# Rotary embedding on one core: the first batch loaded in eight transfers of 16 partitions, and one row of eight moved from TensorE to VectorE

## The chip, the cores and the metric

The kernel runs on one core of a Trainium2 chip. The metric is the device time of one execution in microseconds (us), as the median of several executions. A run is slow when it lies over 1.5% above the fastest of the same kernel.

## The reference, cut to what matters

```python
batch, seq, dim = (16, 512, 1024)            # num_heads = 16, so head_dim 64
x = x.reshape(batch, seq, num_heads, head_dim)
x1, x2 = x[..., :32], x[..., 32:]
rotated = concatenate([x1 * cos - x2 * sin, x1 * sin + x2 * cos], axis=-1)   # fp32
```

The cosine and sine tables are [512, 32]. Input and output are 33.5 MB each, so 67 MB have to move between HBM (the chip's main memory) and SBUF (the core's working memory, 128 partitions), and there is little arithmetic on each byte.

## The kernel before

One batch is one tile: partition p holds the four positions 4p to 4p+3, which is 4096 numbers, 16 KB in one piece of memory. A ring holds ten batches (40 rows of 1024 numbers per partition; "row of work", or unit `u`, below). SyncE issues the loads, ScalarE's queue issues the stores.

```python
PE2 = [u % 2 == 1 for u in range(NU)]        # rows whose two products TensorE adds
V2 = [u % 8 == 3 for u in range(NU)]         # rows whose sine product VectorE makes
# ... (cut)
xv = x.rearrange("b (p r) d -> b p (r d)", r=R)       # R = 4

def on_sync(sp):
    for c in range(NC):
        if c * R >= RING:
            sp.wait_ge(sem_out[c - RING // R], 16)
        sp.dma_start(tile(c), xv[c]).then_inc(sem_in[c], 16)
        if c == 0:
            # the cosine and sine tables, one transfer each (cut)

def on_scalar(ae):
    # tables (cut)
    for u in range(NU):
        c, r, k = where(u)
        if PE2[u]:
            ae.wait_ge(sem_e, n_pe[u])
            ae.activation(xs[:, k, :], t1_ps[:, u % NT1, :], COPY).then_inc(sem_a, 1)
        if r == R - 1:
            wait_added(ae, u)
            ae.dma_start(ov[c], tile(c)).then_inc(sem_out[c], 16)
    for c in range(NC):
        ae.wait_ge(sem_out[c], 16)
```

VectorE multiplies each row of work by the cosine into PSUM (the memory that matmuls add into). GpSimd (VectorE for one row in eight) multiplies the row with its halves swapped by the signed sine into SBUF. The two products are added either by TensorE, as an identity matmul onto the product in PSUM with a copy back by ScalarE, or by VectorE ("comb").

## Time and profile before

| | before |
|---|---|
| median | 162.7 us (162.4 to 163.02, 4 runs) |
| span in the profile | 161.2 us |
| first 16 KB row starts to move | 1.80 us |
| 4096 rows of 611 ns over 16 DMA engines | 156.4 us |
| first load: first row starts, last row ends | 1.80 us, 8.24 us |
| first load, mean of its 128 rows | 717 ns |

A "row" in this table, and in all that follows about transfers, is one 16 KB piece of one partition, the unit in which the DMA engines work here; its times come from the trace's records of single DMA pieces, which do not name the engine. They stand on the clock of the profile. 611 ns a row is 26.8 GB/s for one engine, 429 GB/s for sixteen.

The first two parts of the page of the kernel before. The strings of digits are the busy tenths in 40 slices of 4.03 us; the last line is what the DMA engines moved in each slice:

```profile
span 161.2 us, 678 instructions
PE 83.3 (52%) x134; PEld 27.6 (17%) x134; DVE 122.0 (76%) x108; ACT 34.5 (21%) x35; POOL 130.4 (81%) x62
DVE  0079296998999999969998997976969588796000
POOL 1059999999999999999999993998939989399000
DMA  5999999999999999999999999999999999999995
GB/s 159 404 450 427 427 439 386 398 447 419 431 451 411 439 451 396 451 431 413 447 415 439 443 415 439 447 402 443 423 431 447 411 439 443 413 443 431 419 439 236
```

The engines of the DMA are busy from the second slice to the last but one, while VectorE and GpSimd have holes. So the time is set by the transfers: what counts is when the first row starts, how long each row takes, and whether the engines ever run dry.

The stretches of the first 20 us of the same kernel. The columns are the stretch, its length, the busy time and count of instructions of TensorE's matmuls, TensorE's weight loads, VectorE, ScalarE and GpSimd, the granted clock of TensorE, the DMA share, and GB/s. A row counts whole in the stretch in which it starts, which is why a share can be over 1:

```profile
0.00:5.00 5.00, 2.74 (x6) 0.74 (x6) 0.27 (x1) 1.28 (x1) 0.70 (x6) 1.00 0.66 213
5.00:10.00 5.00, 0.00 (x0) 0.00 (x0) 1.02 (x4) 0.51 (x2) 0.29 (x1) 1.00 1.01 416
10.00:15.00 5.00, 0.49 (x1) 0.50 (x2) 5.00 (x5) 0.00 (x0) 5.00 (x3) 1.00 1.02 436
15.00:20.00 5.00, 5.00 (x7) 1.85 (x6) 2.13 (x3) 1.02 (x1) 5.00 (x3) 1.00 1.01 433
```

The timeline of the start (start, duration, engine, line, operation). The SPq lines are issues of transfers; the first vector copy waits for the cosine table, whose 512-byte pieces start only as the last rows of the first load end (first piece at 7.24 us, last row's end at 8.24 us):

```profile
0.80 0.37 SPq L123 DMA_DIRECT2D x_sb<-in_x_dram  x1
1.22 0.43 SPq L126 DMA_DIRECT2D stage<-in_cos_dram  x1
1.70 0.42 SPq L126 DMA_DIRECT2D stage<-in_sin_dram  x1
8.95 0.29 DVE L202 COPY tab_ps<-stage 128x128 f32<-128x128 f32 x1 [7.75 <-DMA stage<-in_cos_dram]
```

And the end of it, the last copy and the issue of the last store:

```profile
152.35 1.02 ACT L139 ACTIVATE x_sb<-t_ps 128x1024 f32<-128x1024 f32 x1 [5.01 <-PE t_ps L164]
153.41 0.34 ACTq L142 DMA_DIRECT2D out_dram<-x_sb  x1
```

The first row of that store moves at 154.59 us, 1.18 us after the issue began and with no gap behind the store before it: taken in order, its sixteen first rows start within 4 ns of the ends of that store's sixteen last rows. At the start of the kernel the first row moved 1.00 us after its issue began (0.80 to 1.80 us), so the tail has hardly any slack: an estimate from these two is 0.2 us.

### The profile page before, as it was taken

Reading aid. Unit: us, or ns where it says so; the run is one execution under the profiler, and the core shown is the slowest. Engines: PE = TensorE matmul, PEld = TensorE weight load, DVE = VectorE, ACT = ScalarE, POOL = GpSimd, SP = SyncE. Lnnn points to the kernel's source line nnn. Section 1 sums busy time; section 2 is a strip of 40 time slices with the busy share of each in tenths; the row PEclk is TensorE's granted clock in tenths of the full one; section 3 lists DMA queues with packets and bytes.
Section 4 is the critical chain, followed back from the end, with each engine's and each line's share of the span. In section 5 each row is a group of like instructions: output and inputs, shape, how many; then the busy total and the mean of one; then the engine's idle time right before and its main releaser. Section 6 shows DMA issues by size and latency. Waiting matters only on the chain.

```text
span 161.2 us, 678 instructions
## 1 busy us (share of the span) xinstructions
PE 83.3 (52%) x134; PEld 27.6 (17%) x134; DVE 122.0 (76%) x108; ACT 34.5 (21%) x35; POOL 130.4 (81%) x62
## 2 busy tenths in 40 slices
PE   6004949239463665692639444284490784643700
PEld 1002313113121221121212111021120121210100
DVE  0079296998999999969998997976969588796000
ACT  3010222222222222222222222204031203122200
POOL 1059999999999999999999993998939989399000
PEclk9999987995999999579995999959779559789585
DMA  5999999999999999999999999999999999999995
GB/s 159 404 450 427 427 439 386 398 447 419 431 451 411 439 451 396 451 431 413 447 415 439 443 415 439 447 402 443 423 431 447 411 439 443 413 443 431 419 439 236
DMA packets 4900, 67.28 MB, mean 417 GB/s; under 512 B 544, under 2 KB 800, under 8 KB 800
## 3 DMA queue, kind: packets, MB, share of 16 engines
q1 hardware_dynamic: 2592, 33.69, 49.8%
q10 hardware_dynamic: 2304, 33.56, 48.6%
q8 instruction: 1, 0.02, 0.0%
q14 instruction: 3, 0.02, 0.0%
HBM read 33.69 MB, written 33.55 MB: 417 GB/s over the span
## 4 chain that ended last, share of the span: by engine, by line
POOL 27%; DVE 20%; issue 18%; PE 17%; ACT 5%; DMA 5%; another core or an unknown queue 2%; SPq 0%; DVEq 0%; POOLq 0%
POOL t_sb L193 27%; PE t_ps L164 17%; DVE x_sb L235 9%; DVE t_ps L224 8%; DMA stage<-in_sin_dram 5%; ACT x_sb L139 4%; DVE t_sb L215 3%; SPq L126 0%; SPq L123 0%; ACT s_sb L133 0%; ACT s_sb L134 0%; POOLq L115 0%; DVEq L221 0%; DVEq L234 0%
## 5 line engine op out<-in xcount | busy, mean ns | idle before, releaser
L193 POOL TENSOR_TENSOR t_sb<-x_sb,s_sb 128x1024 f32<-128x1024 f32 x56 | 129.7, 2350 | 17.7 <-DMA x_sb<-in_x_dram 9.4
L164 PE MATMUL t_ps<-t_sb,ident 128*128 128x512 f32 x128 | 80.5, 768 | 67.8 <-DVE t_ps L224 46.3
L224 DVE TENSOR_TENSOR t_ps<-x_sb,tab_ps 128x1024 f32<-128x1024 f32 x64 | 76.6, 1226 | 17.1 <-DMA x_sb<-in_x_dram 8.6
L139 ACT ACTIVATE x_sb<-t_ps 128x1024 f32<-128x1024 f32 x32 | 32.7, 1023 | 111.0 <-PE t_ps L164 111.0
L164 PEld LDWEIGHTS t_ps<-t_sb,ident 128*128 128x128 f32 x128 | 26.9, 231 | 120.8 <-DVE t_ps L224 75.9
L235 DVE TENSOR_TENSOR x_sb<-t_ps,t_sb 128x1024 f32<-128x1024 f32 x32 | 39.0, 1218 | 0.0
L215 DVE TENSOR_TENSOR t_sb<-x_sb,tab_ps 128x1024 f32<-128x1024 f32 x8 | 9.7, 1211 | 0.0
L202 DVE COPY tab_ps<-stage 128x128 f32<-128x128 f32 x1 | 0.3, 295 | 7.8 <-DMA stage<-in_cos_dram 7.8
L150 PE MATMUL t_ps<-zero 128*128 128x512 bf16 x6 | 2.7, 630 | 1.3 <-DVE zero L198 1.3
L133 ACT ACTIVATE s_sb<-stage 128x128 f32<-128x128 f32 x1 | 0.3, 309 | 7.0 <-DMA stage<-in_sin_dram 7.0
L133 ACT ACT_TABLE_LOAD x1 | 1.3, 1283 | 0.8 <-PEq L268 0.8
L150 PEld LDWEIGHTS t_ps<-zero 128*128 128x128 bf16 x6 | 0.7, 138 | 2.3 <-DVE zero L198 1.2
L198 DVE MEMSET zero<- 128x256 uint32 x1 | 0.3, 272 | 0.9 <-PEq L268 0.9
L175 POOL MEMSET ident<- 128x128 f32 x1 | 0.2, 204 | 0.3 <-POOLq L268 0.3
L177 POOL TENSOR_SCALAR_AFFINE_SELECT ident<-ident 128x128 f32<-128x128 f32 x1 | 0.3, 292 | 0.1
L268 POOL MEMSET const-float32-0.0<- 128x1 f32 x1 | 0.1, 98 | 0.3 <-issue 0.3
L134 ACT ACTIVATE s_sb<-stage 128x128 f32<-128x128 f32 x1 | 0.3, 293 | 0.0
L204 DVE TENSOR_SCALAR tab_ps<-stage 128x128 f32<-128x128 f32 x1 | 0.3, 284 | 0.0
L205 DVE COPY tab_ps<-stage 128x128 f32<-128x128 f32 x1 | 0.3, 284 | 0.0
L268 POOL MEMSET const-bfloat16-1.0<- 128x1 bf16 x1 | 0.1, 101 | 0.0
L268 POOL MEMSET const-uint8-127<- 128x1 uint8 x1 | 0.1, 101 | 0.0
L268 POOL MEMSET const-float32-1.0<- 128x1 f32 x1 | 0.1, 98 | 0.0
## 6 DMA issues: line engine op xcount, KB each, us to landing
x_sb<-in_x_dram SPq DMA_DIRECT2D x16, 2048.0 KB, 53.6
out_dram<-x_sb ACTq DMA_DIRECT2D x16, 2048.0 KB, 22.1
stage<-in_cos_dram SPq DMA_DIRECT2D x1, 64.0 KB, 7.7
stage<-in_sin_dram SPq DMA_DIRECT2D x1, 64.0 KB, 7.4
```

The costliest lines, as they stand in the source:

```text
L133: ae.activation(s_sb[:, :, 0, :], sv, COPY, scale=-1.0)
L134: ae.activation(s_sb[:, :, 1, :], sv, COPY).then_inc(sem_s, 1)
L139: ae.activation(xs[:, k, :], t1_ps[:, u % NT1, :], COPY).then_inc(sem_a, 1)
L150: pe.matmul(t1_ps[:, k, b * BANK:(b + 1) * BANK], zero[:, 0:P], zero[:], start=True, stop=True).then_inc(sem_w, 1)
L164: ins = pe.matmul(t1_ps[:, u % NT1, b * BANK:(b + 1) * BANK], ident[:], t2[:, b * BANK:(b + 1) * BANK], start=False, stop=True, skip_group ...
L177: pl.affine_select(out=ident[:], in_=ident[:], compare_op=mybir.AluOpType.is_equal, fill=0.0, base=0, pattern=[[-1, P]], channel_multiplier=1,
L193: pl.tensor_tensor(t2_sb[:, u % NT2, :, :, :], swapped(k), sin_of(s_sb, r), mult).then_inc(sem_p, 1)
L198: ve.memset(zero[:], 0.0).then_inc(sem_z, 1)
L215: ve.tensor_tensor(t2_sb[:, u % NT2, :, :, :], swapped(k), sin_of(s_ps, r), mult).then_inc(sem_d, 1)
L224: ve.tensor_tensor(t1_ps[:, u % NT1, :].rearrange("p (h d) -> p h d", d=HALF), x_sb[:, k, :, :, :].rearrange("p h t d -> p (h t) d"), c_ps ...
L235: ve.tensor_tensor(xs[:, k, :], t1_ps[:, u % NT1, :], t2_sb[:, u % NT2, :, :, :].rearrange("p h t d -> p (h t d)"), add,).then_inc(sem_v, 1)
L268: nc = _bacc.Bacc("TRN2", target_bir_lowering=False, num_devices=1)
```

## The change

The intent: in the first load of before, the first rows take 731 to 1944 ns instead of 611. The author's guess was that this comes from engines that start 64 KB or more apart in memory. Cut into eight transfers of 16 partitions, each engine is taken to get one row of each transfer, so that the engines begin 16 KB apart. Rows added by TensorE fall from four of eight to three, so that the last row of every second batch, the last batch among them, no longer passes through TensorE and ScalarE. The sixteen final waits become one, for the ten stores that nothing else waits for.

```diff
-    PE2 = [u % 2 == 1 for u in range(NU)]
+    PE2 = [u % 8 in (1, 3, 6) for u in range(NU)]
...
+    FIRST = 8
...
-                sp.dma_start(tile(c), xv[c]).then_inc(sem_in[c], 16)
-                if c == 0:
+                if c > 0:
+                    sp.dma_start(tile(c), xv[c]).then_inc(sem_in[c], 16)
+                else:
+                    for j in range(FIRST):
+                        ps = slice(j * P // FIRST, (j + 1) * P // FIRST)
+                        sp.dma_start(tile(c)[ps], xv[c, ps]).then_inc(sem_in[c], 16)
...
-                    ae.dma_start(ov[c], tile(c)).then_inc(sem_out[c], 16)
-            for c in range(NC):
-                ae.wait_ge(sem_out[c], 16)
+                    ae.dma_start(ov[c], tile(c)).then_inc(sem_out[c] if c < len(sem_out) else sem_rest, 16)
+            ae.wait_ge(sem_rest, 16 * (NC - len(sem_out)))
...
-                pl.wait_ge(sem_in[c], 16)            # and the same on VectorE
+                pl.wait_ge(sem_in[c], 16 if c else 16 * FIRST)
```

More of the change, by code (lines that the diff above doesn't have):

```diff
@@ L70, in bass_split_heads_rope_kernel @@
         sem_in = [stack.enter_context(nc.semaphore(f"in{c}")) for c in range(NC)]
-        sem_out = [stack.enter_context(nc.semaphore(f"out{c}")) for c in range(NC)]
+        sem_out = [stack.enter_context(nc.semaphore(f"out{c}")) for c in range(NC - RING // R)]
+        sem_rest = stack.enter_context(nc.semaphore("rest"))
         sem_cos = stack.enter_context(nc.semaphore("cos"))
@@ L211, in mul @@
                 if r == 0:
-                    ve.wait_ge(sem_in[c], 16)
+                    ve.wait_ge(sem_in[c], 16 if c else 16 * FIRST)
                 if V2[u]:
```

## The prediction

> **What bounds it now.** The transfers. The page's slice row shows the 16 DMA engines at 9 tenths or more from the second slice to the one before last, at 417 GB/s mean; by stretch, the DMA share is 1.00 to 1.01 from 10 to 154 us. VectorE (122.0 us busy) and GpSimd (130.4 us) have slack overall; the chain of waits names them, but that chain is not the limit while the queues hold work. In the trace's packet records nearly every 16 KB row takes 611 ns; 4096 rows x 611 ns / 16 engines = 156.4 us. The first row starts at 2.2 us, so the floor is near 158.7 us of a 161.2 us span. The other 2.5 us are: (a) the first load, whose 128 rows take 717 ns on average, the very first rows 731 to 1944 ns, which is 0.85 us per engine, about 1.0 on the engine that ended last; (b) the rows read at 24 to 28 us, as the first store begins, about 0.5 us; (c) the rest: table rows, semaphore writes, one engine ending about 1 us after the mean.
>
> **What the change touches.**
> 1. First load in eight: seven more issues at about 0.43 us each (the table issues took 0.42 to 0.43 us on SyncE's queue). One issue feeds each engine a 611 ns row, so issue stays ahead. Aim: remove (a). At most 0.85 to 1.0 us; I expect 0.6 if it works. Added: 7 semaphore writes per engine, 9 ns each, about 0.06 us.
> 2. Rows added by TensorE, from four of eight to three: ScalarE copies fall from 32 to 24, VectorE adds rise from 32 to 40, +8 x 1.22 = +9.8 us, to about 132 us. Per batch VectorE needs about 8.5 us, GpSimd 8.2 us, against 9.7 us of transfer. Still hidden. At the end the last store was issued at 153.41 us, its first row moved about 1.6 us later, just as the engines ran free: hardly 0.2 us of slack. The last row now goes through a VectorE add (1.22 us) instead of a matmul group and copy (3.4 + 1.0 us), so I expect that issue 2 to 3 us earlier, which keeps the tail filled if the start gains.
> 3. One final wait: only the last store's wait counted. About 0.
>
> **The risk.** [...] No run of before shows a 16-partition transfer. I give this a quarter: the rest of the change (freeing the tail) makes sense only if the start gets shorter.
>
> **Prediction.** [...] I say 162.4 us, 8 in 10 within 161.0 to 169.5. Faster by over 2%: 0.02; within 2%: 0.72; slower: 0.26.
>
> **What would show it.** Right: the first load's rows average under 660 ns; table landings near 8 us; DMA share 9 tenths throughout; last store issue near 150.5 us; VectorE near 132 us. Wrong: first-load rows of 1 to 2.4 us for several rounds, a low GB/s in slices 2 to 4, and everything after shifted by the same amount; or VectorE falling behind after 100 us, a hole in the transfers after the last load.

The forecast came to 162.4 us, the upper end of 161.8 to 162.4 us, its range for a first load that isn't slowed.

## The result, and the profile after

The changed kernel takes 174.5 us (174.21 to 174.73, 4 runs) against 162.7 us: a ratio of 1.0724, with a 95% interval from 1.0692 to 1.0756. It is slower by 11.8 us. A ratio in this text is the mean time of one kernel's fast runs over that of the other's of the same rounds, so it isn't quite the ratio of the medians.

The first two parts of the page of the changed kernel, 4.31 us a slice:

```profile
span 172.5 us, 614 instructions
PE 84.1 (49%) x102; PEld 26.0 (15%) x102; DVE 131.4 (76%) x116; ACT 26.4 (15%) x27; POOL 130.3 (76%) x62
DVE  0000195799999997999789997999899969996900
POOL 1000099999999999999999999499884989399100
DMA  8999899999999999999999999999999999999996
GB/s 122 122 122 122 205 429 426 426 429 426 426 426 437 433 429 448 427 426 429 429 427 422 426 441 429 433 445 429 433 429 426 426 426 433 433 429 437 437 429 270
```

Read the last two lines together. The DMA engines count as busy from the start, but in the first four slices they move 122 GB/s instead of about 430. A busy DMA engine isn't a fast one: its row simply takes longer (2092 ns on average in the first load, 717 ns before). Everything after the fifth slice runs at the rate of before.

Its stretches:

```profile
0.00:5.00 5.00, 2.74 (x6) 0.74 (x6) 0.27 (x1) 1.28 (x1) 0.70 (x6) 1.00 0.80 115
5.00:10.00 5.00, 0.00 (x0) 0.00 (x0) 0.00 (x0) 0.00 (x0) 0.00 (x0) 1.00 1.06 125
10.00:15.00 5.00, 0.00 (x0) 0.00 (x0) 0.00 (x0) 0.00 (x0) 0.00 (x0) 1.00 1.09 128
15.00:20.00 5.00, 0.00 (x0) 0.00 (x0) 0.00 (x0) 0.00 (x0) 0.00 (x0) 1.00 0.89 111
```

Its timeline at the start. The eight issues take 3.62 us in all, so issue isn't what holds the first load up; the tables, whose first piece starts at 18.09 us, as the load's last rows end (18.09 to 19.19 us), come 11.9 us later than before (the first copy at 20.83 against 8.95 us):

```profile
0.80 3.62 SPq L131 DMA_DIRECT2D x_sb<-in_x_dram  x8
4.46 0.42 SPq L133 DMA_DIRECT2D stage<-in_cos_dram  x1
4.92 0.43 SPq L133 DMA_DIRECT2D stage<-in_sin_dram  x1
20.83 0.29 DVE L208 COPY tab_ps<-stage 128x128 f32<-128x128 f32 x1 [19.63 <-DMA stage<-in_cos_dram]
```

And its end:

```profile
163.26 1.02 ACT L146 ACTIVATE x_sb<-t_ps 128x1024 f32<-128x1024 f32 x1 [5.05 <-PE t_ps L170]
164.32 0.34 ACTq L149 DMA_DIRECT2D out_dram<-x_sb  x1
```

The trace's records of single rows give the sum. The excess over 611 ns, added up and divided by 16 engines, is the engine time lost:

| engine time lost (us per engine) | before | after |
|---|---|---|
| first load | 0.85 | 11.85 |
| second load | 0.00 | 0.39 |
| fifth load (beside the start of the first store) | 0.53 | 0.01 |
| all rows of the kernel | 1.55 | 12.42 |

The difference of the last line is 10.9 us, of the 11.3 us by which the span grew. From the end of the first load to the end of the span both kernels take nearly the same: 161.22 - 8.24 = 153.0 us before, 172.48 - 19.19 = 153.3 us after. The loss is in the first load. The end of a row's record is not yet its landing: the last semaphore increment of the first load came 0.45 us after it before (8.69 us), and 1.43 us after it in the changed kernel (20.62 us).

### The profile page after: what moved, and what is told of

It is laid out like the page before. It is cut to its first block, busy times and chain, and to the rows that moved or that the text cites. A ratio compares the mean times of both kernels' runs of the same rounds, so it can differ in the third digit from the quotient of the medians.

```text
span 172.5 us, 614 instructions
## 1 busy us (share of the span) xinstructions
PE 84.1 (49%) x102; PEld 26.0 (15%) x102; DVE 131.4 (76%) x116; ACT 26.4 (15%) x27; POOL 130.3 (76%) x62
## 4 chain that ended last, share of the span: by engine, by line
DVE 38%; PE 21%; issue 15%; DMA 9%; ACT 6%; POOL 3%; SPq 2%; DVEq 0%
PE t_ps L170 21%; DVE x_sb L241 18%; DVE t_ps L230 15%; DMA stage<-in_sin_dram 9%; ACT x_sb L146 6%; DVE t_sb L221 4%; POOL t_sb L199 3%; SPq L131 2%; SPq L133 0%; ACT s_sb L140 0%; ACT s_sb L141 0%; DVEq L229 0%; DVEq L240 0%; DVEq L227 0%
## 5 line engine op out<-in xcount | busy, mean ns | idle before, releaser
L230 DVE TENSOR_TENSOR t_ps<-x_sb,tab_ps 128x1024 f32<-128x1024 f32 x64 | 77.0, 1226 | 12.1 <-ACT x_sb L146 10.4
L241 DVE TENSOR_TENSOR x_sb<-t_ps,t_sb 128x1024 f32<-128x1024 f32 x40 | 48.6, 1218 | 0.0
L170 PEld LDWEIGHTS t_ps<-t_sb,ident 128*128 128x128 f32 x96 | 25.3, 289 | 133.4 <-DVE t_ps L230 87.6
L146 ACT ACTIVATE x_sb<-t_ps 128x1024 f32<-128x1024 f32 x24 | 24.6, 1024 | 118.2 <-PE t_ps L170 118.2
L140 ACT ACT_TABLE_LOAD x1 | 1.3, 1283 | 0.8 <-PEq L274 0.8
```

The source lines that it names most:

```text
L140: ae.activation(s_sb[:, :, 0, :], sv, COPY, scale=-1.0)
L170: ins = pe.matmul(t1_ps[:, u % NT1, b * BANK:(b + 1) * BANK], ident[:], t2[:, b * BANK:(b + 1) * BANK], start=False, stop=True, skip_group ...
L230: ve.tensor_tensor(t1_ps[:, u % NT1, :].rearrange("p (h d) -> p h d", d=HALF), x_sb[:, k, :, :, :].rearrange("p h t d -> p (h t) d"), c_ps ...
L241: ve.tensor_tensor(xs[:, k, :], t1_ps[:, u % NT1, :], t2_sb[:, u % NT2, :, :, :].rearrange("p h t d -> p (h t d)"), add,).then_inc(sem_v, 1)
```

## The experiments

Four theories stood at first. **A**: the set of partitions to which a load writes at one time sets how long its rows take, whether these are neighbours or not (the prediction's risk). **B**: engines that read memory 16 KB apart get in each other's way in HBM. **C**: eight small transfers cost more than one, in issues and semaphore writes. **D**: the limit is per block of neighbouring partitions.

This table is the core of the evidence, from the row records: the mean row of the first load in ns, by rounds of 16 rows in order of their start.

| kernel | how the first load is cut | round 1 | round 2 | round 4 | round 8 |
|---|---|---|---|---|---|
| before | whole | 1307 | 705 | 621 | 613 |
| after | 8 x 16 neighbouring partitions | 1378 | 2159 | 2199 | 2201 |
| e3_rows_apart | the same, memory 128 KB apart | 1209 | 2013 | 2052 | 2052 |
| e4_stride4 | 8 x every fourth partition, memory as in after | 1014 | 1068 | 1183 | 1190 |
| e6_four32 | 4 x 32 neighbouring partitions | 992 | 1213 | 1283 | 1281 |
| e7_two64 | 2 x 64 neighbouring partitions | 830 | 1212 | 1273 | 1275 |

### e1_whole: undo the cut, keep the rest

```diff
-    FIRST = 8
+    FIRST = 1
```

> The changed kernel with its first load put back into one transfer of 128 partitions; the row split (three of eight) and the single final wait stay. Every theory that blames the way the first load is cut expects the time of before, 162.7 us within 0.5, first-load rows near 717 ns. If the row split or the single wait cost something of their own, this run stays above 163.5 us. If the freed tail is worth anything, it is up to 0.5 us under before.

Measured: 162.39 us (5 runs) against 162.59 us, ratio 0.9984 (0.9972 to 0.9997). The cut alone makes the loss. The row split and the single wait together are worth 0.16%, and the run doesn't tell which of the two gives it. It is the fastest version of all, but by so little that it counts as the same. Its GB/s line and its last issue:

```profile
GB/s 143 404 453 424 436 436 367 432 441 408 453 420 432 445 412 438 428 428 449 402 449 432 420 449 412 441 432 416 453 424 428 441 408 453 424 428 449 404 449 281
152.38 0.34 ACTq L149 DMA_DIRECT2D out_dram<-x_sb  x1
```

The start is that of before. The last store is issued at 152.38 us, 1.0 us earlier than before, not the 2 to 3 us of the prediction. The last row of the batch no longer waits for TensorE, but the row before it still does: its matmuls (3.68 us, from 147.61 us) and the copy after them, which ends at 152.35 us, now come last.

### e2_only_eight: the cut alone, on the kernel before

```diff
-                sp.dma_start(tile(c), xv[c]).then_inc(sem_in[c], 16)
+                    for j in range(8): ...     # as in the change; waits for 16 * 8 on batch 0
```

> The kernel before with only the first load cut into eight transfers of 16 partitions. If the cut alone makes the loss: 174.5 us within 0.7, first-load rows near 2100 ns. If the loss needs the fuller VectorE too, clearly less, 165 to 172 us.

Measured: 174.32 us (4 runs), ratio 1.072 (1.0701 to 1.0739), rows of the first load 2101 ns on average. The loss is there without the row split.

### e3_rows_apart: the same partitions, other memory addresses

```diff
-                        sp.dma_start(tile(c)[ps], xv[c, ps]).then_inc(sem_in[c], 16)
+                        sp.dma_start(tile(c)[ps], xv[c, j::FIRST]).then_inc(sem_in[c], 16)
```

> The changed kernel, eight transfers to the same blocks of 16 partitions, but each fetches every eighth row of memory, so the engines read 128 KB apart instead of 16 KB (batch 0 comes out wrong on purpose). Theory A[...]: nothing changes, rows near 2200 ns, 174.5 us. Theory B, engines that read 16 KB apart collide in HBM: rows fall to 620 to 750 ns, about 163 us. Theory C, cost of many small transfers: 174.5 us.

Measured: 173.15 us once, rows at 2052 ns (batch 0 wrong). Theory B falls: with 128 KB between the engines' addresses the rows are 7% shorter, not 70%. In this one trace addresses have a small part in it; the partitions hold the large one. Its GB/s line starts as slowly as that of the changed kernel:

```profile
GB/s 122 126 122 120 297 429 429 425 432 436 436 432 432 432 429 432 432 427 429 429 427 429 429 432 429 432 432 429 432 432 432 440 429 432 432 432 429 432 432 264
```

### e4_stride4: the same memory addresses, other partitions

```diff
-                        sp.dma_start(tile(c)[ps], xv[c, ps]).then_inc(sem_in[c], 16)
+                        p0 = 64 * (j // 4) + j % 4
+                        sp.dma_start(tile(c)[p0:p0 + 61:4], xv[c, ps]).then_inc(sem_in[c], 16)
```

> The changed kernel, eight transfers that read the same memory as in the changed kernel (16 rows in a row each) but write to every fourth partition of one half: partitions 0,4,..,60 and so on (batch 0 wrong on purpose). Theory A: [...] half the time per row: about 1100 ns, first load near 9 us, total about 166 us. Theory B and theory C: 2200 ns and 174.5 us as before this edit. Theory D, a limit per block of 16 neighbouring partitions: four blocks in use, so full rate, rows near 620 ns, about 163 us.

Measured: 166.45 us once, first load from 2.17 to 11.92 us, rows 1139 ns on average and 1190 ns in the last round (batch 0 wrong). This is theory A's number. B and C wanted 2200 ns, D wanted 620 ns. Together with e3, memory and partitions are changed one at a time, and the time follows the partitions. The GB/s line, which reaches the full rate two slices earlier than in the changed kernel:

```profile
GB/s 143 227 219 415 438 422 414 446 438 422 430 430 442 426 426 426 440 438 418 418 444 442 418 430 426 446 430 426 418 446 442 418 414 446 442 418 434 426 438 263
```

### e5_columns: eight transfers over all partitions

```diff
-                        ps = slice(j * P // FIRST, (j + 1) * P // FIRST)
-                        sp.dma_start(tile(c)[ps], xv[c, ps]).then_inc(sem_in[c], 16)
+                        cs = slice(j * R * dim // FIRST, (j + 1) * R * dim // FIRST)
+                        sp.dma_start(tile(c)[:, cs], xv[c, :, cs]).then_inc(sem_in[c], 16)
```

> The changed kernel with its first load in eight transfers again, but each of all 128 partitions and an eighth of every row (2 KB pieces). Theory A[...]: [...] full rate, total 162.7 us within 0.8. Theory C (the number of transfers and issues, with eight semaphore writes per engine instead of one): 170 us or more, as the count is the same as in the changed kernel and the pieces are smaller.

Measured: 163.52 us (4 runs), ratio 1.0051 (1.0033 to 1.0069). Theory C falls as an account of the loss: eight issues and eight semaphore writes per engine cost 0.8 us, not 11.8, and they cost it here with smaller pieces. A 2 KB piece takes 84 ns at the median, so 1024 of them need 5.38 us per engine where 16 KB rows need 4.89, and the pieces lost another 1.6 us to uneven rates. The GB/s line has no slow start:

```profile
GB/s 136 323 406 425 441 429 417 441 417 437 441 417 437 437 421 435 433 425 433 435 425 433 437 425 429 441 425 429 441 421 433 441 421 433 441 421 433 429 344 324
```

### e6_four32 and e7_two64: larger blocks

```diff
-    FIRST = 8
+    FIRST = 4          # e6_four32; 2 in e7_two64
```

> The changed kernel with FIRST = 4: four transfers of 32 neighbouring partitions. Theory A: [...] rows near 1150 ns, as with every fourth partition, total near 166.5 us. Theory C: half the transfers, half the loss: total near 168.5 us.

> The changed kernel with FIRST = 2: two transfers of 64 neighbouring partitions. Theory A [...] no better than FIRST = 4: rows near 1150 ns, total near 166.5 us. Theory D (a limit per block of neighbouring partitions) and theory C: close to the whole load, rows under 800 ns, total 163 to 164.5 us.

Measured: 166.59 us and 167.03 us, once each. The GB/s lines, e6_four32 first:

```profile
GB/s 155 227 190 415 446 390 438 446 446 402 426 446 446 426 402 448 438 442 410 424 438 446 434 402 442 442 442 402 434 442 446 426 406 442 446 438 398 442 442 271
```

```profile
GB/s 139 206 199 396 433 436 425 425 433 436 440 409 436 433 436 440 403 440 436 433 438 409 436 436 436 440 409 433 440 436 429 417 436 440 437 417 429 436 401 298
```

Twice the partitions of the changed kernel give not quite twice the rate (about 206 GB/s, worked out as 16 rows in 1272 ns, the median row of both), and 64 give no more than 32: both first loads last 10.08 us. Where one transfer took 6.44 us for the first load, two of 64 partitions took those 10.08 us, and the kernel took 4.3 us more than the one before on the same chip (167.03 against 162.71). That 64 are no better than 32 is the strangest of theory A's forecasts, and it holds; no run shows the reason. What the runs show is the time of a row by the set of partitions, in the last round: 2201 ns for 16 neighbours; 1190 ns for every fourth of 64, 1281 for 32 neighbours, 1275 for 64 neighbours; 613 ns for all 128 in one transfer. Theory D falls, since 64 neighbouring partitions would have been nearly free. The sharpest test is missing: no run sent a transfer to 16 partitions spread over all 128.

### e8_view: the aim without the cost

One transfer of 128 partitions, but with the sequence laid out so that neighbouring groups of four partitions begin 16 KB apart (FIRST = 1 as well):

```diff
+                        sp.dma_start(
+                            tile(c).rearrange("p (r d) -> p r d", r=R),
+                            x[c].rearrange("(r p) d -> p r d", r=R),
+                        ).then_inc(sem_in[c], 16)
```

> The aim of the change without its cost: one first load over all 128 partitions, but with the sequence split so that partition p gets positions p, p+128, p+256, p+384, in pieces of 4 KB; engines with neighbouring groups of four partitions then begin 16 KB apart (batch 0 wrong on purpose). If the slow first rows of before (1307 ns on average in the first round, 0.85 us lost per engine) come from engines that begin 64 KB or more apart, this load loses under 0.3 us per engine. If they come from sixteen streams starting at once, whatever their addresses, the loss stays near 0.85 us and the total at 162.6 us.

Measured: 162.69 us once (batch 0 wrong). The 4 KB pieces took 159 ns at the median, and the excess over that was 0.37 us per engine, between the two forecasts, and less than the 0.85 us of before. But 512 pieces of 159 ns need 5.09 us per engine, 0.20 us more than the rows of 16 KB, so the first load ended no earlier (8.31 us, 8.24 before). Whether spacing or piece size shortened the first round isn't settled. What this one run shows is the size of the prize: well under 1 us, and none of it arrived.

### e9_last_store: the same cut on a store

```diff
+                        for j in range(8):
+                            ps = slice(j * P // 8, (j + 1) * P // 8)
+                            ae.dma_start(ov[c, ps], tile(c)[ps]).then_inc(sem_out[c], 16)   # last batch only
```

> The kernel before with its last store, not its first load, cut into eight transfers of 16 partitions. [...] rows of the last store near 2200 ns, total near 174 us. If only writes to SBUF are limited: rows stay near 611 ns and the total near 163 us.

The condition of the first forecast was that the store is slowed as the load was. Measured: 166.68 us once (the run of before beside it 162.52 us), rows of that store 1116 ns on average, from 611 to 1864. In this run the store is slowed too, but it lost 4.0 us per engine, not 11. Neither forecast had this, and why this store lost less stays open.

### e10_mid and e12_second: the same cut on a later load

```diff
-                if c > 0:
+                if c != 5:         # e10_mid: batch 5 is cut; c != 1 in e12_second
```

> The changed kernel with the first load whole and the sixth load (batch 5) cut into eight transfers of 16 partitions, in the stretch where loads and stores alternate on every engine. Theory A with no way to make up lost engine time: the same loss as at the start, 11 us, total near 174 us, rows of that load near 2200 ns. If the store rows in between keep the engines apart or fill the waits: clearly less, 165 to 171 us. If only the start of the kernel is sensitive: near 162.5 us.

Measured: 168.57 us once (beside 162.52). The rows of the cut load took 1036 ns on average (3.4 us lost per engine), and the store rows beside it 778 ns (2.2 us). Half the loss, then. Two things were different from the start of the kernel: stores lay between the loads, and the engines came to it spread out in time. e12_second has the second without the first:

> The changed kernel with the first load whole and the second load (batch 1) cut into eight transfers of 16 partitions. No store is in flight yet, as in the changed kernel, but the engines come to it after eight rows each, spread over about a row's time instead of 0.3 us. If entering spread out is what made the loss smaller in the cut sixth load: rows well under 2200 ns, 1000 to 1700, total 166 to 171 us. If the store rows in between did it: rows near 2200 ns, total near 174 us.

Measured: 173.69 us once (beside 162.62). The rows of the cut load's first round took 611 to 2038 ns, and from its third round on every row took 2013 to 2026 ns. The engines came to it over 0.51 us, less than the forecast's row time and less than the 1.26 us of e10_mid, but the first round's rows ended over 1.94 us, and the rows after them were slow all the same. So a spread alone isn't what helped; with no stores in between, the engines settled into the slow pattern by themselves in this run. The one difference left in e10_mid that was looked for is the store rows in between; how they help isn't shown. The GB/s line of e12_second, slow from the third slice on:

```profile
GB/s 175 408 122 130 134 183 427 439 435 435 431 427 427 427 431 431 425 427 431 431 441 423 435 435 435 431 427 431 427 431 431 427 427 435 427 439 427 435 355 362
```

### e11_two_queues: half of the cut on the other queue

```diff
-                    for j in range(FIRST):
+                    for j in range(FIRST // 2):      # the other four from ScalarE's queue
```

> The changed kernel, but of the eight first transfers the four of partitions 64 to 127 are issued from ScalarE's queue[...]. If an engine works on one row at a time, whatever the queue: still about 2200 ns a row and 174.5 us. [...] the first load takes about half, 9 us, total near 166 us.

SyncE's queue has partitions 0 to 63, ScalarE's 64 to 127. The condition of the second forecast was that an engine held up on a row of one half can move a row of the other half through its second queue. Measured: 174.1 us once, rows of the two halves at 2180 to 2254 ns from the second round on. Its GB/s line begins as that of the changed kernel:

```profile
GB/s 122 122 122 122 182 433 441 429 425 425 429 425 425 437 425 433 433 431 444 425 429 424 425 433 433 429 437 437 437 425 429 425 425 433 437 429 433 433 401 308
```

In this run the second queue didn't shorten the rows: from one queue, in the changed kernel, they took 2159 to 2201 ns from the second round on.

## Why the prediction was wrong

The measured 174.5 us lies 12.1 us above the 162.4 us forecast, and beyond the 169.5 us at the top of its 8 in 10. The prediction counted on first-load rows under 660 ns; they took 2092 ns on average.

- **What bounds the kernel: right.** The 10.9 us of engine time lost, nearly all of it in one load, came back in the span (11.3 us), because the transfers bound it.
- **"I give this a quarter: the rest of the change (freeing the tail) makes sense only if the start gets shorter": this step failed.** A risk that had been seen was set against a guess about the purpose of an edit, and the guess was given three quarters. In place of the 0.6 us gain that this put first, the slow first load came: 119 GB/s in it (16 rows in 2200 ns), where rows of 611 ns give 429. By e3, e4, e6 and e7 the time goes with the partitions written (2052, 1190, 1281 and 1275 ns a row in the last round); the mechanism isn't shown.
- **The size of the loss.** It measured 11.0 us (11.85 - 0.85). The engines don't drift apart. In the changed kernel the ends of the first round's rows lie between 2.72 and 3.81 us, those of the eighth between 18.09 and 19.19 us: a spread of 1.09 us at first and 1.10 us at last, and each row takes 2.2 us for whoever is ahead or behind. Whoever came first to the next transfer's partitions gained nothing by it: the shortest row after the first round took 2142 ns. Why isn't settled. The whole load took 17.4 us.
- **"I expect 0.6 if it works": no.** In the changed kernel the first round took 1378 ns, no better than the 1307 ns of before. In e8, one transfer over all 128 partitions in 4 KB pieces, the excess fell from 0.85 to 0.37 us, and smaller pieces ate part of it.
- **VectorE near 132 us, hidden: right.** It measured 131.4 us, and e1, with the split in it, is no slower than before.
- **The last issue 2 to 3 us earlier: 1.0 us** in e1, as the last TensorE row of the batch became the last to finish.
- **One final wait, about 0: not contradicted.** e1 gives both edits together 0.2 us.

## What to carry to other kernels

Cut a transfer along the bytes of a partition rather than along the partitions: here eight pieces of all 128 partitions cost 0.8 us, and eight pieces of 16 partitions each cost 11.8 us. When the DMA line of a profile says busy, look at the GB/s line too, since the engines were "busy" at 122 GB/s for 17 us. And when a risk of an edit has been seen and no run has measured it, don't discount it because the edit seems to have a purpose; a few edits that agree with each other show that somebody had a theory, not that it holds.
